# A softmax in one pass: stores moved to ScalarE's own transfer queue, loads made 64 KB a row

## Chip, cores and metric

One core of one Trainium2 chip. The metric is the device time of one execution in microseconds (us). Repeats of the kernel before differ by 0.1 to 1.4 us within a set of runs, and its medians by 0.7 us between the five sets. Each ratio to the kernel before is from runs of the same rounds on one chip. The sets are: the result itself; e1 to e4; m1 and m2; e5, e6 and e8; e9, e10 and m3. Where the text compares two changed kernels of different sets, it compares across chips too, and says so.

## The reference

```python
def reference(logits, temperature):          # (16, 256, 32768) float32, temperature 1.0
    scaled = logits / temperature
    scaled = scaled - scaled.max(axis=-1, keepdims=True)
    exp_scaled = np.exp(scaled)
    return exp_scaled / exp_scaled.sum(axis=-1, keepdims=True)
```

536.87 MB are read and 536.87 MB written. Each row of 32768 is split over two partitions, so there are G = 64 tiles of 128 partitions x 16384 elements: 64 KB a partition, 8.39 MB a tile.

## The kernel before

Three whole-tile buffers rotate. The SyncE queue carries everything, in this order: store of tile t, load of tile t + 2. Compute works in place: maxima on VectorE, exp with row sums on ScalarE, small combining steps, then the scaling, shared by VectorE and ScalarE.

```python
_BUFS = 3
_LOAD = 8192          # columns of one load:  32 KB a partition, two loads a tile
_STORE = 16384        # columns of one store: 64 KB a partition
...
_END = 4096           # first and last tile: pieces of 16 KB a partition
...
    def load(t):
        n = _END if t in (0, G - 1) else _LOAD
        for s in range(0, W, n):
            nc.sync.dma_start(out=buf[t % _BUFS][:, s : s + n], in_=x[t * P : (t + 1) * P, s : s + n])

    def store(t):
        n = _END if t == G - 1 else _STORE
        for s in range(0, W, n):
            nc.sync.dma_start(out=o[t * P : (t + 1) * P, s : s + n], in_=buf[t % _BUFS][:, s : s + n])
...
        for t in range(_BUFS):
            load(t)
        for t in range(G):
            normalise(t)
            store(t)
            if t and t + _BUFS - 1 < G:
                load(t + _BUFS - 1)
```

Of the kernel before, what the change touches and what calls it, by code (L numbers as in the profile page):

```python
# [1 line left out]

# [4 lines left out]


_SPLIT = 2
_BUFS = 3  # L10
_LOAD = 8192
_STORE = 16384
_PIECES = (4096, 4096, 4096, 2048, 2048)
_ON_DVE = (4096, 4096, 2048, 0, 0)
_END = 4096
_END_ON_DVE = 2560
_SETS = 3


@with_exitstack  # L20
def kernel(
    ctx: ExitStack,
    tc: tile.TileContext,
    logits: bass.AP,
    temperature: bass.AP,
    out: bass.AP,
):
    nc = tc.nc
    inv_t = 1.0 / float(temperature)
    P = nc.NUM_PARTITIONS  # L30
    fp32 = mybir.dt.float32
    Exp = mybir.ActivationFunctionType.Exp
    Copy = mybir.ActivationFunctionType.Copy
    X = mybir.AxisListType.X
    A = mybir.AluOpType

    xf = logits.flatten_outer_dims()
    of = out.flatten_outer_dims()
    N, V = xf.shape
    W = V // _SPLIT  # L40
    assert sum(_PIECES) == W and len(_PIECES) == len(_ON_DVE)
    x = xf.rearrange("n (h v) -> (n h) v", h=_SPLIT)
    o = of.rearrange("n (h v) -> (n h) v", h=_SPLIT)
    G = N * _SPLIT // P
    assert G * P == N * _SPLIT
    n_rounds = _SPLIT.bit_length() - 1
    K = max(len(_PIECES), W // _END)

    pool = ctx.enter_context(tc.tile_pool(name="fixed", bufs=1))
    buf = [pool.tile([P, W], fp32, tag=f"x{b}", name=f"x{b}") for b in range(_BUFS)]  # L50
    widths = dict(nm=K, ssum=K, ee=K, f=K, ttj=K, nMh=2, Sh=2, rS=1)
    stat = [
        {
            k: pool.tile([P, w], fp32, tag=f"{k}{s}", name=f"{k}{s}")
            for k, w in widths.items()
        }
        for s in range(_SETS)
    ]

    def load(t: int) -> None:  # L60
        n = _END if t in (0, G - 1) else _LOAD
        for s in range(0, W, n):
            nc.sync.dma_start(  # L63
                out=buf[t % _BUFS][:, s : s + n],
                in_=x[t * P : (t + 1) * P, s : s + n],
            )

    def store(t: int) -> None:
        n = _END if t == G - 1 else _STORE
        for s in range(0, W, n):  # L70
            nc.sync.dma_start(  # L71
                out=o[t * P : (t + 1) * P, s : s + n],
                in_=buf[t % _BUFS][:, s : s + n],
            )

    def combine(v, op) -> None:
        for j in range(n_rounds):
            mask = [i ^ (1 << j) for i in range(32)]
            nc.vector.stream_shuffle(  # L79
                out=v[:, j + 1 : j + 2], in_=v[:, j : j + 1], mask=mask  # L80
            )
            nc.vector.tensor_tensor(  # L82
                out=v[:, j + 1 : j + 2],
                in0=v[:, j : j + 1],
                in1=v[:, j + 1 : j + 2],
                op=op,
            )

    def normalise(t: int) -> None:
        xs = buf[t % _BUFS]  # L90
        if t in (0, G - 1):
            sizes = [_END] * (W // _END)
            on_dve = [_END_ON_DVE] * len(sizes)
        else:
            sizes, on_dve = _PIECES, _ON_DVE
        K = len(sizes)
        at = [sum(sizes[:k]) for k in range(K)]
        st = stat[t % _SETS]
        nm, ssum, ee, f, ttj = (st[k][:, :K] for k in ("nm", "ssum", "ee", "f", "ttj"))
        nMh, Sh, rS = st["nMh"], st["Sh"], st["rS"]  # L100
        for k in range(K):
            xc = xs[:, at[k] : at[k] + sizes[k]]
            nc.vector.tensor_reduce(  # L103
                out=nm[:, k : k + 1], in_=xc, axis=X, op=A.max, negate=True
            )
            if inv_t != 1.0:
                nc.vector.tensor_scalar_mul(
                    out=nm[:, k : k + 1], in0=nm[:, k : k + 1], scalar1=inv_t
                )
            nc.scalar.activation(  # L110
                out=xc,
                in_=xc,
                func=Exp,
                bias=nm[:, k : k + 1],
                scale=inv_t,
                accum_out=ssum[:, k : k + 1],
            )
        nc.vector.tensor_reduce(out=nMh[:, 0:1], in_=nm, axis=X, op=A.min)  # L118
        combine(nMh, A.min)
        nc.scalar.activation(  # L120
            out=ee, in_=nm, func=Exp, bias=nMh[:, n_rounds : n_rounds + 1], scale=-1.0
        )
        nc.vector.tensor_tensor_reduce(  # L123
            out=ttj,
            in0=ee,
            in1=ssum,
            scale=1.0,
            scalar=0.0,
            op0=A.mult,
            op1=A.add,  # L130
            accum_out=Sh[:, 0:1],
        )
        combine(Sh, A.add)
        nc.vector.reciprocal(out=rS, in_=Sh[:, n_rounds : n_rounds + 1])  # L134
        nc.vector.tensor_scalar_mul(out=f, in0=ee, scalar1=rS)  # L135
        for k in range(K):
            a, b, c = at[k], at[k] + on_dve[k], at[k] + sizes[k]
            if b > a:
                nc.vector.tensor_scalar_mul(  # L139
                    out=xs[:, a:b], in0=xs[:, a:b], scalar1=f[:, k : k + 1]  # L140
                )
            if c > b:
                nc.scalar.activation(  # L143
                    out=xs[:, b:c], in_=xs[:, b:c], func=Copy, scale=f[:, k : k + 1]
                )

    with tc.manual_schedule():
        for t in range(_BUFS):
            load(t)
        for t in range(G):  # L150
            normalise(t)
            store(t)
            if t and t + _BUFS - 1 < G:
                load(t + _BUFS - 1)


# [1 line left out]
_INS = ['logits', 'temperature']  # L158
_OUTS = [((16, 256, 32768), 'float32')]

_NUMBERS = {'temperature': 1.0}


# [26 lines left out]
```

## Time and profile before

| | before |
|---|---|
| time, median of 4 | 2495.82 us (2495.76 to 2495.86) |
| span in the profile | 2494.7 us |
| VectorE / ScalarE busy | 63% / 55% |
| transfers busy, on one queue | 99.7% |
| mean rate | 430 GB/s |

The bytes set the time. The rows of the windows view that the later comparison needs: the first 215 us, the stretch of them from 40 to 100 us, the middle and the end (columns: window, its length, busy us of VectorE, ScalarE and GpSimd with instruction counts, clock, share of the transfer engines, GB/s):

```profile
0.00:215.00 215.00, 142.72 (x112) 123.97 (x82) 0.20 (x4) 1.00 1.00 427
...
40.00:100.00 60.00, 47.20 (x38) 42.70 (x28) 0.00 (x0) 1.00 1.01 428
...
215.00:2376.00 2161.00, 1372.62 (x1050) 1183.53 (x775) 0.00 (x0) 1.00 1.00 433
...
2454.90:2494.70 39.80, 11.65 (x16) 13.29 (x9) 0.00 (x0) 1.00 0.69 294
```

From 40 to 100 us the rate is already 428 GB/s, within about 1% of the 433 of the middle.

### The profile page before, as it was taken

The numbers are of one execution on the slowest core, as the hardware profiler recorded it, in microseconds if no ns is written. First come the engines' busy times: TensorE is split into PE (matmuls) and PEld (weight loads), VectorE is DVE, ScalarE is ACT, GpSimd is POOL, SyncE is SP. The second block draws the span as 40 slices with busy tenths as digits, with TensorE's granted clock in tenths as the row PEclk, the third lists the DMA queues.
The fourth block names the chain that finished last, engine by engine and source line by source line (L and its number), as shares of the span: only waits on it lengthen the run. The fifth ranks groups of instructions, "written<-read, shape, count | busy, mean of one in ns | idle before, by whom it ended". The sixth has DMA issues, their size and how long they took to land.

```text
span 2494.7 us, 2743 instructions
## 1 busy us (share of the span) xinstructions
DVE 1581.4 (63%) x1216; ACT 1367.8 (55%) x895; POOL 0.2 (0%) x4
## 2 busy tenths in 40 slices
DVE  7666566665765657656666566665766656666574
ACT  6555464554645546455464554645646556465463
POOL 0000000000000000000000000000000000000000
DMA  9999999999999999999999999999999999999998
GB/s 420 428 427 438 426 435 435 430 438 430 431 435 433 437 434 426 439 429 435 439 425 438 428 436 436 428 439 431 433 433 433 438 432 430 433 433 434 437 426 350
DMA packets 28678, 1073.93 MB, mean 430 GB/s; under 512 B 3184, under 2 KB 3184, under 8 KB 3184
## 3 DMA queue, kind: packets, MB, share of 16 engines
q1 hardware_dynamic: 28656, 1073.75, 99.7%
q14 instruction: 22, 0.18, 0.0%
HBM read 536.87 MB, written 536.87 MB: 430 GB/s over the span
## 4 chain that ended last, share of the span: by engine, by line
DMA 73%; ACT 13%; DVE 12%; another core or an unknown queue 1%; SPq 1%; issue 0%; ACTq 0%
DMA x<-in_logits_dram 64%; DVE nm L103 11%; DMA out_dram<-x 8%; ACT x L110 7%; ACT x L143 6%; SPq L71 0%; DVE f L135 0%; ACT ee L120 0%; DVE rS L134 0%; DVE Sh L82 0%; DVE ttj L123 0%; DVE Sh L79 0%; SPq L63 0%; ACTq L185 0%
## 5 line engine op out<-in xcount | busy, mean ns | idle before, releaser
L103 DVE TENSOR_REDUCE nm<-x 128x1 f32<-128x4096 f32 x318 | 1123.3, 3581 | 673.3 <-DMA x<-in_logits_dram 673.3
L110 ACT ACTIVATE x<-x,nm 128x4096 f32<-128x4096 f32 x318 | 965.4, 3036 | 1020.9 <-DVE nm L103 1020.9
L143 ACT ACTIVATE x<-x,f 128x2048 f32<-128x2048 f32 (+1 forms) x194 | 370.9, 1975 | 73.7 <-DVE f L135 73.7
L139 DVE TENSOR_SCALAR x<-x,f 128x4096 f32<-128x4096 f32 (+2 forms) x194 | 372.2, 1975 | 2.3
L123 DVE CUSTOM_DVE_ANT_0 ttj<-ee,ssum 128x5 f32<-128x5 f32 (+1 forms) x64 | 10.6, 166 | 196.7 <-ACT ee L120 196.7
L110 ACT ACTIVATION_READ_ACCUMULATOR x<-x,nm 128x1 f32 x318 | 59.3, 186 | 0.0
L120 ACT ACTIVATE ee<-nm,nMh 128x5 f32<-128x5 f32 (+1 forms) x64 | 18.1, 284 | 0.0
L135 DVE TENSOR_SCALAR f<-ee,rS 128x5 f32<-128x5 f32 (+1 forms) x64 | 14.8, 231 | 2.2
L134 DVE RECIPROCAL rS<-Sh 128x1 f32<-128x1 f32 x64 | 10.5, 164 | 2.2
L82 DVE TENSOR_TENSOR nMh<-nMh 128x1 f32<-128x1 f32 x64 | 10.2, 159 | 2.2
L82 DVE TENSOR_TENSOR Sh<-Sh 128x1 f32<-128x1 f32 x64 | 10.2, 159 | 2.2
L118 DVE TENSOR_REDUCE nMh<-nm 128x1 f32<-128x5 f32 (+1 forms) x64 | 10.1, 158 | 2.2
L79 DVE STREAM_SHUFFLE nMh<-nMh 128x1 f32<-128x1 f32 x64 | 9.7, 151 | 0.0
L79 DVE STREAM_SHUFFLE Sh<-Sh 128x1 f32<-128x1 f32 x64 | 9.7, 151 | 0.0
L110 ACT ACT_TABLE_LOAD x1 | 1.3, 1283 | 8.1 <-DMA x<-in_logits_dram 8.1
L123 DVE DVE_READ_ACCUMULATOR2_ANT Sh<- 128x1 f32 x64 | 5.3, 82 | 0.0
L79 DVE LOAD_MASK_SELECT Sh<-Sh x64 | 0.9, 14 | 2.8
L79 DVE LOAD_MASK_SELECT nMh<-nMh x64 | 0.9, 14 | 2.8
L171 POOL MEMSET const-bfloat16-1.0<- 128x1 bf16 x1 | 0.1, 102 | 0.0
L171 POOL MEMSET const-uint8-127<- 128x1 uint8 x1 | 0.1, 102 | 0.0
L171 POOL MEMSET const-float32-1.0<- 128x1 f32 x1 | 0.1, 99 | 0.0
L171 POOL MEMSET const-float32-0.0<- 128x1 f32 x1 | 0.1, 98 | 0.2 <-issue 0.2
## 6 DMA issues: line engine op xcount, KB each, us to landing
x<-in_logits_dram SPq DMA_DIRECT2D x124, 4096.0 KB, 48.9
x<-in_logits_dram SPq DMA_DIRECT2D x8, 2048.0 KB, 31.8
out_dram<-x SPq DMA_DIRECT2D x4, 2048.0 KB, 18.0
out_dram<-x SPq DMA_DIRECT2D x63, 38.6
```

The lines of the kernel that those rows point to most:

```text
L79: nc.vector.stream_shuffle(out=v[:, j + 1 : j + 2], in_=v[:, j : j + 1], mask=mask)
L82: nc.vector.tensor_tensor(out=v[:, j + 1 : j + 2], in0=v[:, j : j + 1], in1=v[:, j + 1 : j + 2], op=op,)
L103: nc.vector.tensor_reduce(out=nm[:, k : k + 1], in_=xc, axis=X, op=A.max, negate=True)
L110: nc.scalar.activation(out=xc, in_=xc, func=Exp, bias=nm[:, k : k + 1], scale=inv_t, accum_out=ssum[:, k : k + 1],)
L118: nc.vector.tensor_reduce(out=nMh[:, 0:1], in_=nm, axis=X, op=A.min)
L120: nc.scalar.activation(out=ee, in_=nm, func=Exp, bias=nMh[:, n_rounds : n_rounds + 1], scale=-1.0)
L123: nc.vector.tensor_tensor_reduce(out=ttj, in0=ee, in1=ssum, scale=1.0, scalar=0.0, op0=A.mult, op1=A.add, accum_out=Sh[:, 0:1],)
L134: nc.vector.reciprocal(out=rS, in_=Sh[:, n_rounds : n_rounds + 1])
L135: nc.vector.tensor_scalar_mul(out=f, in0=ee, scalar1=rS)
L139: nc.vector.tensor_scalar_mul(out=xs[:, a:b], in0=xs[:, a:b], scalar1=f[:, k : k + 1])
L143: nc.scalar.activation(out=xs[:, b:c], in_=xs[:, b:c], func=Copy, scale=f[:, k : k + 1])
L171: nc = _bacc.Bacc("TRN2", target_bir_lowering=False, num_devices=1)
```

## The change

The intent: give the stores a queue of their own, so that a load need not be issued behind a store that waits for compute, and halve the number of rows that the loads consist of. Two smaller things go with it: the loads stand one tile earlier in the program, and the last tile's stores are issued piece by piece between its scalings.

```diff
-_LOAD = 8192
-_STORE = 16384
+_LOAD = 16384
...
-    def store(t: int) -> None:
-        n = _END if t == G - 1 else _STORE
-        for s in range(0, W, n):
-            nc.sync.dma_start(
-                out=o[t * P : (t + 1) * P, s : s + n],
-                in_=buf[t % _BUFS][:, s : s + n],
-            )
+    def store(t: int, a: int, b: int) -> None:
+        nc.scalar.dma_start(
+            out=o[t * P : (t + 1) * P, a:b], in_=buf[t % _BUFS][:, a:b]
+        )
...
+            if t == G - 1:
+                store(t, a, c)          # last tile: piece by piece, behind each scaling
+        if t < G - 1:
+            store(t, 0, W)
...
             normalise(t)
-            store(t)
-            if t and t + _BUFS - 1 < G:
-                load(t + _BUFS - 1)
+            if t + _BUFS < G:
+                load(t + _BUFS)
```

## The prediction

> **What bounds the kernel now.** I read the page from the top: busy shares, the 40 slices, the queues, then the chain of waits.
>
> ```profile
> span 2494.7 us, 2743 instructions
> DVE 1581.4 (63%) x1216; ACT 1367.8 (55%) x895; POOL 0.2 (0%) x4
> ...
> DMA packets 28678, 1073.93 MB, mean 430 GB/s; under 512 B 3184, under 2 KB 3184, under 8 KB 3184
> ...
> q1 hardware_dynamic: 28656, 1073.75, 99.7%
> q14 instruction: 22, 0.18, 0.0%
> ...
> DMA 73%; ACT 13%; DVE 12%; another core or an unknown queue 1%; SPq 1%; issue 0%; ACTq 0%
> ```
>
> The reader is to see that the transfers are busy for 99.7% of the span while the two compute engines rest for 37% and 45% of it. The tensor is read once and written once, 1073.74 MB, and that is what sets the time. The chain of waits gives 12% and 13% to the compute engines, but it names the last event, not the scarce one: the order of issues below shows why.
>
> Next the timeline of SyncE's issues, late in the run:
>
> ```profile
> 2318.36 0.34 SPq L71 DMA_DIRECT2D out_dram<-x  x1
> 2319.30 0.80 SPq L63 DMA_DIRECT2D x<-in_logits_dram  x2
> 2358.03 0.34 SPq L71 DMA_DIRECT2D out_dram<-x  x1
> 2358.42 0.91 SPq L63 DMA_DIRECT2D x<-in_logits_dram  x2
> 2396.72 0.34 SPq L71 DMA_DIRECT2D out_dram<-x  x1
> 2397.11 1.86 SPq L63 DMA_DIRECT2D x<-in_logits_dram  x4
> 2435.41 35.36 SPq L71 DMA_DIRECT2D out_dram<-x  x5
> ```
>
> One tile (8.39 MB in, 8.39 MB out) passes every 38.69 us (2396.72 less 2358.03), or 39.67 us in some (2358.03 less 2318.36). 16.78 MB in 38.70 us is 433.5 GB/s. The store of tile 3 was issued at 140.90 and that of tile 62 at 2435.41: 59 periods, 2294.5 us, 11.2 us more than 59 x 38.70.
>
> Then VectorE's waits for the loads, in its timeline:
>
> ```profile
> 2406.34 8.74 DVE L103 TENSOR_REDUCE nm<-x 128x1 f32<-128x4096 f32 x2 [9.68 <-DMA x<-in_logits_dram]
> 2416.03 8.81 DVE L103 TENSOR_REDUCE nm<-x 128x1 f32<-128x4096 f32 x3 [0.95 <-DMA x<-in_logits_dram]
> ...
> 2445.10 4.42 DVE L103 TENSOR_REDUCE nm<-x 128x1 f32<-128x4096 f32 x1 [0.44 <-DMA x<-in_logits_dram]
> 2449.98 4.42 DVE L103 TENSOR_REDUCE nm<-x 128x1 f32<-128x4096 f32 x1 [0.46 <-DMA x<-in_logits_dram]
> ```
>
> A 4 MB load lands 9.69 us after its forerunner, a 2 MB one 4.88 us. And the windows view over the end, from the 62nd store's issue to the end of the span (columns: window, length, busy us by engine, clock, DMA share, GB/s):
>
> ```profile
> 2435.30:2494.70 59.40, 25.01 (x20) 21.45 (x14) 0.00 (x0) 1.00 0.81 347
> ```
>
> By the landings, one load and two stores, 25.2 MB, were still to come at 2435; but only 347 GB/s x 59.4 us = 20.6 MB moved. So the mean engine had run some 4.6 MB, or 10 us, ahead of the engine that lands last. My reading: one of the 16 transfer engines also fetches the instructions (22 packets, 0.18 MB) and loses those 11.2 us; it alone sets every landing, and the rest wait for it at the end.
>
> **What the Trainium skill says.** "DMA: Bandwidth & Descriptors", section "Where 436 GB/s comes from", puts the ceiling at 435.2 GB/s; the 433.5 of this trace agree. In "Issuing engines are not separate DMA queues" it says that transfers started by different engines run on the same 16 engines and interleave, so that a second issuer saves only issue time; the kernel before has one issuer and cannot show it. In "Queues, rings and completion order" it says that each engine takes turns between its queues packet by packet; no run so far shows that for two data queues. In "Why small descriptors are slow" it gives some 3 cycles of overhead for a packet. The trace is of that order: at 435.2 GB/s 4.194 MB take 9.637 us, the landing distance is 9.69, and 0.053 us over the 8 rows and one completion of each engine are 5.9 ns each.
>
> **The change part by part.**
>
> Rows of 64 KB in the loads. The 62 middle tiles (all but the first and the last) lose 8 rows and one completion on each engine: 9 x 5.9 ns = 0.053 us a tile, times 62 = 3.3 us saved. The bytes stay. The price is that a tile's first maximum waits for the whole tile. Compute from a whole tile to its last scaling took 27.96 us for tile 1 (maxima from 38.08, scaling over at 66.04). A buffer's round of three periods is 116.1 us. If the two queues share evenly, a load and a store take 38.7 us each, and 116.1 - 38.7 - 38.7 - 28.0 = 10.7 us are left for latencies. The first load of 2 MB was issued at 0.73 and landed at 8.03: 7.3 us, less 4.88 of moving, is 2.4 us of latency. Two such, 4.9 us, fit in 10.7. So in the middle at least one queue always has work, and the transfers stay full: cost 0.
>
> Issues on ScalarE. 63 whole tiles and 4 pieces: 67 at 0.34 us = 23 us on an engine that is idle for 1127 us; each stands behind the scaling of its tile, where ScalarE would wait some 4.4 us for VectorE's next maximum anyway. Cost 0. SyncE no longer holds the load back behind the store's wait for compute, but that wait is now 0.39 us, with a load of 19 us still queued: worth 0.
>
> Interleaving. Before, the queue goes in phases: 8 MB in, 8 MB out, two turns a tile. After, an engine alternates a 64 KB row in and one out: 16 turns. What does a turn cost? The phases alone predict 2 x 9.69 + 19.33 (a store at the same rate) = 38.71 against 38.70 measured, so a turn costs nothing within about 0.02 us. 14 more turns at 0.02 would be 0.3 us a tile, 18 us in all, as an upper edge; I take 0 as the likely value.
>
> The start. Tile 0 comes in four pieces as before. The rest of load 1 now shares with store 0, so compute of tile 1 starts a few us later, but loads or stores are queued throughout: 0.
>
> The end. Before, load 63 stands ahead of store 62, and store 62 (19.3 us) covers the compute of the last tile: the last piece lands at 2454.9, the first scaling is over at 2465.9, while store 62 moves until about 2474. Afterwards store 62 shares with load 63. Worked from the landing of load 62 (time 0): store 61 has about 17 us of work left, load 63 19.3. Load 63 comes in rows of 16 KB, the stores in rows of 64 KB. If turns go row by row, the store gets four fifths: store 61 is out at 21, the load has had 4.3; alone until store 62 begins at about 30, it gets to 13; the next 24 us give 4.8 more while store 62 leaves; the load lands at about 55-56 with nothing left to move. Then the compute of the last piece is bare: 4.42 (maximum) + 3.7 (exp) + 0.3 + 1.3 (small steps) + 1.5 (scaling) + 1.9 (issue to bytes) = 13 us of idle transfers. If turns are fair by bytes, the load lands at about 39 with 16 us of store 62 left, and nothing is bare. I give the first two chances in three: 0.65 x 13 = +8.5 us.
>
> Sum: 2495.8 - 3.3 + 8.5 + 0 = 2501; the turn between directions may as well hide some of the 5.9 ns a row (27 a tile, 64 tiles, 10 us at most) as cost something. I put it at 2500.
>
> **The rivals.** (1) *Two queues run faster* because reads and writes overlap. For it: nothing seen here. Against it: 433.5 of 435.2 GB/s is already reached, and even with every overhead and the 11.2 us of instruction fetch gone, the bytes alone are 2467 us: -1.1%. It would give 2470 to 2485. (2) *A turn between queues or directions costs*. For it: the 22 instruction packets, which come from another queue, lose 11.2 us, 0.51 us each, where 8 KB at 27.2 GB/s are 0.30: 0.2 us for a visit of two turns. If that were the price of leaving a queue, 16 turns a tile at 0.1 would be 1.6 us, +4%, about 2600. Against it: small packets to another target may be slow by themselves, and the phases show a free turn of direction. (3) *The whole-tile load leaves bubbles*: if latencies under load eat more than the 10.7 us, each tile shows a gap; 1 us a tile would make 2560. Against it: landings follow each other without gaps now, with one queue deep in work. (4) *The end stays covered*: 2492.
>
> **Range and chances.** The core is 2490 to 2505: bytes fixed, the end worth 0 to +13, rows worth -3. Below it 2484 needs hidden overheads; above it, 2535 allows 0.5 us a tile for turns or bubbles. Faster by over 2% would need 2446, less than the bytes take at the ceiling: 0.01. Slower by over 2% (2546) needs rival 2 or 3: 0.08. Within: 0.91.
>
> **What would show it.** Right: periods between stores of 38.6 to 38.7 us; the queues' two shares near 50% each, sum near 99%; time to landing of loads and stores both near 38 us; about 19,750 packets (17,536 rows, 137 x 16 completions, 22 of instructions); VectorE waiting for a load once a tile; in the last 40 us a trough of the transfers before the last stores. Wrong: periods over 39.2 us with the transfers still "busy" (turns cost), or slices below 9 in the middle (bubbles); a span under 2484 (overheads hidden); ScalarE's exp waiting behind its own issue.

## The result, and the profile after

The changed kernel took 2514.82 us, median of 4 runs (2512.59 to 2516.96), against 2495.82 us. The ratio is 1.0076 with a 95% interval of 1.0059 to 1.0094: slower by 0.8%, inside the band called the same. The profiled run, the quickest of the four, has a span 16.0 us longer than before.

The page of the changed kernel, the parts that answer to those shown of before:

```profile
span 2510.7 us, 2617 instructions
DVE 1575.7 (63%) x1216; ACT 1368.1 (54%) x895; POOL 0.2 (0%) x4
...
DMA packets 19748, 1073.91 MB, mean 428 GB/s; under 512 B 2192, under 2 KB 2192, under 8 KB 2192
...
q1 hardware_dynamic: 10080, 536.88, 49.7%
q10 hardware_dynamic: 9648, 536.88, 49.6%
q14 instruction: 20, 0.16, 0.0%
...
out_dram<-x ACTq DMA_DIRECT2D x63, 44.3
x<-in_logits_dram SPq DMA_DIRECT2D x62, 43.6
```

The two queues share almost evenly, and the compute engines are as busy as before. Loads and stores each take some 44 us from issue to landing; the prediction had named 38. Nothing else here shows where 16 us went. The windows do:

```profile
0.00:215.00 215.00, 125.81 (x96) 108.05 (x70) 0.20 (x4) 1.00 0.99 409
...
40.00:100.00 60.00, 33.33 (x22) 25.15 (x16) 0.00 (x0) 1.00 0.97 368
...
215.00:2376.00 2161.00, 1376.00 (x1064) 1195.63 (x784) 0.00 (x0) 1.00 1.00 433
...
2470.00:2490.00 20.00, 8.62 (x14) 6.40 (x5) 0.00 (x0) 1.00 0.07 28
```

**The start.** By 215 us the changed kernel had moved 409 x 215 = 87.9 MB, the kernel before 427 x 215 = 91.8 MB. 3.9 MB at 433 GB/s are 9 us. The loss sits between 40 and 100 us, where load 2 and store 0 run side by side at 368 GB/s although both queues have work: load 2 lands at 91.3 us and store 0 at 91.4.

The kept trace also has a record of every packet, with its queue, start and duration, though no view prints them; here a packet of data is one row. Between 40 and 92 us a load's row of 64 KB took 2.94 us in the mean and a store's 2.59, against a median of 2.42 for both in the middle. So the engines were not idle: the rows themselves took longer.

**The middle.** 433 GB/s, as in the kernel before.

**The end.** For 20 us the transfers all but stop (28 GB/s). Before, the mean engine also lost time at the end, 39.8 us x (1 - 294/433) = 12.8 us after 2454.9 us, where, by the prediction's reading, the other engines waited for the one that lands last; after, the same sum over the last 41 us gives 18.7 for the trough and 20.7 us x (1 - 393/433) = 1.9 for what follows, 20.6 us in all. So the end costs about 8 us more, and 9 + 8 = 17 answers to the 16.0 us of the spans within rounding.

VectorE's timeline of the changed kernel at the end, the waits for loads 62 and 63:

```profile
2419.97 17.46 DVE L99 TENSOR_REDUCE nm<-x 128x1 f32<-128x4096 f32 x5 [10.51 <-DMA x<-in_logits_dram]
...
2447.85 13.06 DVE L99 TENSOR_REDUCE nm<-x 128x1 f32<-128x4096 f32 x3
2477.43 4.42 DVE L99 TENSOR_REDUCE nm<-x 128x1 f32<-128x4096 f32 x1 [16.51 <-DMA x<-in_logits_dram]
```

Load 62 landed at 2420.0. Two pieces of load 63 were there at 2448 and the third at 2452.7, but the fourth landed at 2477.4, beside store 62 (issued at 2448.0, landed 29.6 us later, at 2477.6). The timeline merges the first three pieces' maxima into one line. With nothing left to move, the last piece's compute ran bare until the first store of the last tile was issued at 2488.8.

### The profile page after: what moved, and what is told of

Read it like the earlier page. It is cut to its first block, busy times and chain, and to the rows that moved or that the text cites. A ratio compares the mean times of both kernels' runs of the same rounds, so it can differ in the third digit from the quotient of the medians.

```text
span 2510.7 us, 2617 instructions
## 1 busy us (share of the span) xinstructions
DVE 1575.7 (63%) x1216; ACT 1368.1 (54%) x895; POOL 0.2 (0%) x4
## 4 chain that ended last, share of the span: by engine, by line
DMA 72%; DVE 17%; ACT 9%; another core or an unknown queue 2%; issue 0%; SPq 0%; ACTq 0%
DMA x<-in_logits_dram 36%; DMA out_dram<-x 35%; DVE nm L99 12%; ACT x L106 7%; DVE x L135 4%; ACT x L139 2%; DVE f L131 0%; ACT ee L116 0%; DVE rS L130 0%; DVE Sh L78 0%; DVE ttj L119 0%; DVE Sh L75 0%; SPq L62 0%; ACTq L68 0%
## 6 DMA issues: line engine op xcount, KB each, us to landing
out_dram<-x ACTq DMA_DIRECT2D x63, 44.3
```

## The experiments

Twelve runs. "Period" is the distance of one tile's store issue from the next.

**e1_rows_only**: the load size alone, on one queue.

```diff
-_LOAD = 8192                       # in the kernel before
+_LOAD = 16384
```

> The kernel before with one load of 64 KB rows a tile, all on SyncE's queue as before. Theory: the rows alone are worth 9 packets x 5.9 ns = 0.053 us a tile, 3.3 us in all, and one queue keeps the phases apart, so neither the slow start (40 to 100 us) nor the trough at the end appears: 2492.5 us, ratio 0.9985 to 0.9995. Rival (the whole-tile load is what costs: compute starts later and leaves bubbles): 2505 to 2515.

Measured: median 2501.74 us, ratio 1.0026 (1.0001 to 1.0050), but the four runs were 2496.4, 2497.4, 2506.1 and 2509.9, where the kernel before stayed within 2495.8 to 2496.4. In the profiled run (span 2495.6) many periods are 38.63 to 38.66 us, against 38.69 to 38.72 before: the 0.06 us that the rows were to save is there. But stretches of 38.8 to 39.4 come between, and eat it. So neither expectation holds as it stands: longer rows bring a small gain and an unsteady loss, with one queue too.

**e2_queue_only**: the second queue alone, loads of 32 KB rows, stores of 64 KB.

```diff
-_LOAD = 16384                      # in the changed kernel
+_LOAD = 8192
```

> The changed kernel with loads of 32 KB rows, so only the second queue is left of the change. Theory (turns are taken row by row): the stores' 64 KB rows get two thirds while both queues have work, so a store lands some 33 us after its issue instead of 44; the slow start and the trough at the end stay, and the time is 2515 to 2522. Rival (turns are fair by bytes): landing stays near 44 us.

Measured: 2637.8 us, ratio 1.0568 (1.0539 to 1.0597). A miss by 115 us. The shares are those of turns taken row by row:

```profile
x<-in_logits_dram SPq DMA_DIRECT2D x124, 4096.0 KB, 51.4
...
out_dram<-x ACTq DMA_DIRECT2D x63, 35.5
```

The stores land 9 us sooner than in the changed kernel (35.5 against 44.3). Landing times alone would fit any turns of equal numbers of rows, a whole transfer's eight rows on an engine, say. The packet records decide it. They do not name the engine, but a row's end can be matched to the next row's start: in the middle of the changed kernel the queue changes after some 85% of the rows so matched, where turns of eight rows could give at most one change in eight. The turn is one row.

But e2's periods run from 27.9 us to 68.6, and the middle moves at 412 GB/s. Why, m3 below takes up.

**e3_end_rows**: the last stores in the rows of the last load.

```diff
         if t < G - 1:
-            store(t, 0, W)
+            n = _END if t >= G - 3 else W
+            for s in range(0, W, n):
+                store(t, s, s + n)
```

> The changed kernel with the stores of tiles 61 and 62 cut into four transfers of 16 KB rows each, the same rows as the last load has. Theory (row by row): the last load gets half and not a fifth, lands some 39 us after load 62 with most of store 62 still to move, and the trough before the last stores goes: 13 us less than the changed kernel, about 2501. Rival (the end is bare whatever the rows, since store 62 runs beside the load and not behind it): trough stays, 2513 to 2517.

Measured: 2500.90 us, 13.9 us less than the changed kernel by the medians and 11.9 by the profiled spans (different sets); ratio to before 1.0025 (1.0008 to 1.0041). The windows show the trough mostly closed, from 20 us at 28 GB/s to:

```profile
2460.00:2470.00 10.00, 4.15 (x5) 10.00 (x6) 0.00 (x0) 1.00 1.01 433
2470.00:2480.00 10.00, 5.56 (x11) 7.88 (x8) 0.00 (x0) 1.00 0.37 155
2480.00:2490.00 10.00, 1.26 (x1) 2.48 (x2) 0.00 (x0) 1.00 0.99 419
```

Nothing but the cut of two stores into shorter rows changed, and the packet records show turns of one row, so the bare end of the changed kernel comes from turns taken row by row: 64 KB for store 62 against 16 KB for load 63.

**e4_start_sp**: the stores of tiles 0 and 1 on SyncE's queue, in the order of before.

```diff
-        nc.scalar.dma_start(
+        q = nc.sync if t < 2 else nc.scalar
+        q.dma_start(
...
-            if t + _BUFS < G:
-                load(t + _BUFS)
+            if t and t + _BUFS - 1 < G:
+                load(t + _BUFS - 1)
```

> The changed kernel with the stores of tiles 0 and 1 on SyncE's queue, in the order of the kernel before, so that no store runs beside the loads of the start. Theory (at the start loads and stores that begin together with all engines in step cost about 9 us, between 42 and 91 us of the changed kernel): 2505 to 2508, and the windows from 40 to 140 us show 425 GB/s and more. Rival (a first stretch of mixed traffic is always slow, whenever it begins): the slow stretch only moves to about 120 to 180 us and the time stays 2513 to 2517.

Measured: 2522.46 us, ratio 1.0106 (1.0090 to 1.0121). The theory failed. The rival was right that the stretch moves, to where the first store on the second queue now runs; but the stretch got longer, and the time is 5 us above the rival's range too:

```profile
40.00:100.00 60.00, 49.13 (x38) 42.71 (x28) 0.00 (x0) 1.00 0.99 420
100.00:140.00 40.00, 0.00 (x0) 0.00 (x0) 0.00 (x0) 1.00 1.00 378
140.00:215.00 75.00, 58.00 (x41) 46.68 (x31) 0.00 (x0) 1.00 0.96 404
```

**m1_copy_one and m2_copy_two**: bare copies: `normalise(t)` is replaced by `store(t, 0, W)`; in m1 the store is on `nc.sync` and the order that of before. Their outputs are wrong, which doesn't matter for the times.

> A bare copy (wrong result on purpose): the same loads of 64 KB rows and stores, no compute, one queue on SyncE. Theory: pure rate 434 GB/s, about 2475 us, since there are few instructions to fetch and so no engine falls behind; periods all alike. Rival: periods of 39.7 us stay, then instruction fetch is not their cause.

> The same bare copy (wrong result on purpose) with stores on ScalarE's queue and loads on SyncE's. Theory (mixing is free except for a slow stretch after the first common start): 2475 to 2490 us, windows after 150 us at 433 GB/s, some slow windows at the start. Rival (mixing costs all along, hidden in the changed kernel by its compute phases): under 425 GB/s throughout, over 2520 us.

Measured: m1 2487.83 us, m2 2501.16 us (2 runs each). In m1 the periods after 1016 us and up to the end of the middle are all between 38.60 and 38.70. The jumps to 39.67 us that the kernel before has every six or seven tiles are gone, with 2 instruction packets where that one has 22. But m1 has no compute either, so it does not settle the cause by itself. The packet records of the kernel before do: each of its nine jumps begins 0.5 to 0.7 us after an 8 KB fetch packet of 0.31 us, behind which a row took 0.56 to 0.65 us longer than its like. Together that is nearly the whole 0.97 us. (Its other fetch packets delay a row less, and no jump follows.) m1 still missed its 2475 by 13 us: its first 19 periods, 81.9 to 822.1 us, average 38.96 us, the unsteadiness of e1 again. In m2 mixed traffic of 64 KB rows ran at 425 GB/s between 40 and 100 us and at 434 after 215 us. So mixing two queues need not be slow, and a first common start need not be either. m2 missed its range, 2475 to 2490, as well: its 13 us over m1 are again a bare end, 74 GB/s from 2460 to 2470 us.

**e5_both_ends**: e3, and the store of tile 0 in 16 KB rows too.

```diff
-            n = _END if t >= G - 3 else W
+            n = _END if t == 0 or t >= G - 3 else W
```

> The kernel of e3_end_rows with the store of tile 0 cut into four transfers of 16 KB rows as well. If turns go row by row, load 2 then gets four fifths and lands near 66 us instead of 91, and load 3 waits for store 0 until some 82 us. Theory (the start is slow only because load 2 and store 0, with rows alike, begin together on all engines and stay in step): no slow stretch, 8 to 10 us less than e3, about 2492. Rival (any first mixing is slow, as e4 suggests): the stretch only moves, 2498 to 2503.

Measured: 2496.84 us (2494.6 to 2503.4), ratio to before 1.0014 (0.9997 to 1.0031): 4 us less than e3 by the medians, 6.0 by the profiled spans. The two are of different sets, with spreads of 8 and 9 us, and the intervals of their ratios overlap, so the gain in time is not clear of noise. What the trace does show is that the slow stretch is gone, and not moved:

```profile
40.00:100.00 60.00, 49.12 (x38) 42.64 (x28) 0.00 (x0) 1.00 1.00 428
100.00:140.00 40.00, 14.98 (x5) 9.51 (x6) 0.00 (x0) 1.00 1.03 444
140.00:215.00 75.00, 47.29 (x39) 40.85 (x28) 0.00 (x0) 1.00 1.00 433
```

By 215 us e5 was some 9 us ahead of e3 (429 against 411 GB/s over this stretch); in the profiled runs 3 of them are lost again, by the packet records in the middle.

**e6_start_late**: e3, with store 0 meant to start half a tile later.

> The kernel of e3_end_rows with the store of tile 0 issued behind the first exp of tile 1, some 11 us later, when load 2 has moved half its rows; rows of 64 KB in both. Theory (being in step is what is slow): 40 to 100 us move at 420 GB/s and more, 8 to 10 us less than e3, about 2492. Rival (the first mixing is slow whatever the phase): the stretch stays under 390 GB/s, 2498 to 2503.

This one failed, by my mistake. I placed `store(0)` behind the first exp of tile 1, and in program order that is behind load 3, which overwrites the same buffer. So the store waited for load 3 (its issue came at 80.7 us and not near 49), and it wrote tile 3's data: a wrong result. It is no test of the phase between load and store. (2497.15 us.) Its trace still shows one thing: the slow rows, with 394 GB/s from 100 to 140 us, are those of load 4, and the first of them (2.68 us in the mean from 120 to 130 us) ran before any store ran beside them.

**e8_rows_32**: two queues, 32 KB rows on both sides.

```diff
-_LOAD = 16384
+_LOAD = 8192
...
-            store(t, 0, W)
+            for s in range(0, W, _LOAD):
+                store(t, s, s + _LOAD)
```

> The changed kernel with rows of 32 KB on both sides (each load and each store in two transfers), against the unequal rows of e2. Theory (unequal rows on the two queues are what cost e2 its 140 us): equal rows bring the periods back to about 38.7 us, 2510 to 2525. Rival (two queues with 32 KB rows are slow by themselves): over 2600, with periods as irregular as in e2.

Measured: 2505.86 us, 4 us below the theory's range, both runs within 0.12 us; ratio 1.0041. 40 to 100 us at 431 GB/s, periods 38.67 to 38.73 with the same jumps to 39.7 as before. The bare end is left: the transfers stand still from 2470 to 2480 us, for store rows of 32 KB still outweigh load rows of 16 KB there.

**e9_store_32**: the mirror of e2: stores of 32 KB rows, loads of 64 KB.

```diff
-            store(t, 0, W)
+            for s in range(0, W, 8192):
+                store(t, s, s + 8192)
```

> The changed kernel with only the stores cut to rows of 32 KB (two transfers a tile), loads left at 64 KB: the mirror of e2. Theory (the slow stretches need 64 KB rows in the stores that run beside loads): no slow stretch at 40 to 140 us and even periods, 2500 to 2510. Rival (unequal rows as such cost, by feeding one queue twice as fast as the other until the fed one is empty): over 2560 and irregular periods as in e2, only with the loads ahead.

Measured: 2502.99 us (2 runs), ratio 1.0028. 40 to 100 us at 428 GB/s. The time and the start are as the theory said, but the periods are not even, 37.3 to 39.9 in the middle, and a trough stays at the end (85 GB/s from 2470 to 2480 us). The shares turn round: loads now land 33.6 us after their issue. Unequal rows as such do not cost 5%.

**e10_rows_32_end**: e8 with equal rows at the end too.

```diff
-            for s in range(0, W, _LOAD):
+            n = _END if t >= G - 3 else _LOAD
+            for s in range(0, W, n):
```

> e8 (32 KB rows on both sides, two queues) with the stores of the last three tiles in 16 KB rows, as the last load has. Theory (with equal rows throughout, two queues cost nothing and give nothing): no slow start, no trough, 2494 to 2497, within 2 us of the kernel before and with its small spread. Rival (a second queue still costs at the end, since store 62 no longer stands behind load 63): 2500 and more.

Measured: 2495.06 us (2494.5 to 2495.5), ratio 0.9996 (0.9979 to 1.0012), correct. It equals the kernel before. With rows of 32 KB in the middle and of equal length at the end, a second queue costs nothing and brings nothing. No version beat the kernel before by more than the noise.

**m3_copy_unequal**: m2 with the rows of e2.

```diff
-_LOAD = 16384                      # in m2
+_LOAD = 8192
```

> A bare copy (wrong result on purpose) on two queues with the rows of e2: loads of 32 KB, stores of 64 KB, no compute. Theory (in e2 the transfers themselves are not slower; the stores' two thirds starve the loads, tiles come in bunches and the fast engines run out of queued work while VectorE computes): without compute nothing can bunch, 2495 to 2520. Rival (this mix of rows is slow on the engines themselves): 2600 and more without any compute.

Measured: 2608.51 us (2 runs), ratio to before 1.0450 where m2 has 1.0020 (different sets): 107 us more than m2, without any compute. The rival was right:

```profile
140.00:215.00 75.00, 0.00 (x0) 1.00 1.00 434
215.00:2376.00 2161.00, 0.00 (x0) 1.00 1.00 414
```

The first tiles run at full rate. Then the engines are busy all the time (share 1.00) and still move only 414 GB/s: the rows themselves take longer, by the packet records 1.27 us for a load's 32 KB and 2.53 for a store's 64 KB in the mean, against 1.21 and 2.42 at full rate. So e2's bunched tiles are not needed for most of its loss.

## Why the prediction was right or wrong

The measured 2514.8 us lies inside the stated range, 2484 to 2535, and "within 2%" was right. But the forecast was 4 us of loss and 19 came; the range held because it had been left wide for turns and bubbles, not because the loss was seen. Step by step:

- **What bounds the kernel: right.** The transfers stayed 99% busy and the compute engines' times did not move. Rivals 1 (two queues faster) and 3 (bubbles in the middle) did not happen: 433 GB/s in the middle of both kernels.
- **The engine that lags from instruction fetch: supported.** Each of the nine jumps of 0.97 us follows a fetch packet, and m1, with 2 such packets, has none after 1016 us. That it is always the same engine is not in the trace.
- **Rows, -3.3 us: right in size, not in effect.** e1 and m1 show 38.64 us against 38.70, 0.06 us a tile or 3.7 us in all. What the step left out is that 64 KB rows in the loads make other stretches slower and the time uncertain by up to 13 us (e1).
- **The issue on ScalarE, 0: right.** ScalarE's busy time is 1368.1 us against 1367.8 before, and e10, which issues its stores there too, takes the time of before.
- **The end, +8.5 us as two thirds of 13: the mechanism right, the size that of its first branch.** Predicted from the landing of load 62: store 61 out after 21 us, load 63 in after 55 to 56. Measured: 21.4 us (2409.5 + 31.9 = 2441.4, less 2420.0) and 57.5 us. From the last landing (2477.4) to the first bytes of the last tile's stores (issue 2488.8 plus the latency taken there, 1.9) is 13.3 us. e3 took it away and gained 13.9 us. So 4.8 us of the miss are the weight I gave to turns that are fair by bytes. By the bytes of the two profiled runs the end costs only 8 us net, since the end of the kernel before idles too; that this is near my 8.5 is luck.
- **The start, 0: wrong.** This is the step that failed. "Loads or stores are queued throughout: 0" is true of the queues, but a full queue was taken for a full rate. Between 40 and 100 us the mixed rows moved at 368 GB/s against 428 before, and by 215 us 9 us had gone.
- **A turn between directions costs nothing: right in the middle, wrong as a general rule.** Its evidence was two turns a tile in one queue. Alternation row by row also ran at full rate in the middle of the changed kernel, in e8 and in e10. Yet the start of the changed kernel and of e4, and m3 from some 320 us on, were slow. There the rows lengthened; that the turns did it (rival 2) is not shown. In m3 it is unlikely: loads that followed another load took longer (1.29 us) than those that followed a store (1.23).

The sum with these terms is 2495.8 - 3.7 + 13.3 + 9 = 2514.4. It is no test: the 3.7 us come from e1 and m1, and the middle of the changed kernel shows hardly any of them. The sounder account is the one by bytes above, 9 us at the start and 8 at the end against 16.0 between the spans.

**What stays open** is why rows get slow in such stretches. Shown is what goes with them: the stretch at the start vanished when store 0 (e5) or all stores (e8, e9, e10) had shorter rows, and moved with the first store on the second queue (e4); stores of 64 KB beside loads of 32 KB are slow for most of the run even without compute (m3); the reverse is not (e9). But 64 KB rows on both queues are not enough by themselves, as the start of m2 and the middle of the changed kernel show, and e1 has milder slow stretches on one queue. Nor are loads and stores in flight at the same moment what it takes: in m3 after 215 us the rows at whose midpoint no row of the other queue was in flight were the slowest, 6.5% over the full-rate time, and e6 has slow loads with no store beside them. That it depends on how far the 16 engines are in step would fit, but my test of it (e6) failed, and it was only argued.

## What to carry to other kernels

When one queue already kept the transfers at their full rate, a second one added no bytes (433 GB/s in the middle of both kernels); it replaces an order that you chose (load ahead of store) by turns, and the lengths of the rows on both sides then decide who is served. Before the last tiles, make sure that the load whose compute comes last is not starved by a store that could have covered it, either by order or by equal rows. A full queue is not a full rate: look at GB/s by window, and at the spread of repeats, before longer rows are called a gain.

## What the Trainium skill lacked or had wrong

- "DMA: Bandwidth & Descriptors", section "Issuing engines are not separate DMA queues", says that a second issuer only saves issue time. Here the second queue also changed the rate and the order: with loads of 32 KB rows and stores of 64 KB, two queues took 2637.8 us (e2), and without compute 2608.5 us (m3), against 2495.9 us for the same rows on one queue.
- The same page, "Queues, rings and completion order", describes the packet between two turns as several descriptors. In these runs the turn was one row: the queue changed after some 85% of the matched rows of the changed kernel, and stores landed after 35.5 us beside loads of half the row (e2), after 44.3 us beside loads of the same row, and the loads after 33.6 us beside stores of half the row (e9).
- "Runtime: NRT & Kernel Launch" has a section on instruction fetch, but neither it nor any other page that I read says what the fetch does to a kernel bound by transfers: here one tile in six or seven was 0.97 us longer, each behind a fetch packet, and none in the steady part of m1, with 2 fetch packets for 22.
- No page that I read warns of rows of 64 KB, instead of 32, in the loads as well: they saved 0.06 us of 38.70 a tile, and made repeats of one kernel differ by 13.6 us (e1) where the kernel before differed by 0.6.
